# A squared-ReLU MLP by Strassen-Winograd products: two pairs interleaved in the first layer, the second layer's products taken over both token halves, sums and stores moved between queues

## The chip, the cores and the metric

The kernel runs on one core of a Trainium2 chip. The metric is the device time of one execution in microseconds (us), the median over the runs. A core has TensorE (PE, with its weight loads as PEld), VectorE (DVE), ScalarE (ACT), GpSimd (POOL) and SyncE (SP), which only issues DMAs. Each engine works through its own instructions in order; one that waits holds up all behind it. An engine that issues DMAs does so in the same order, among its other work.

## What is computed

One decoder layer over 2048 tokens of width 1024, in float32: three token mixers side by side, an output projection with residual, then an MLP, then a final norm. The change lies in the MLP and in the hand-over to it:

```python
        x = x + jnp.concatenate([ya, yb, yc], axis=-1) @ w_out[i]
        h = rmsnorm(x, norm2_g[i])
        x = x + jnp.square(jax.nn.relu(h @ w_ff1[i])) @ w_ff2[i]
    return rmsnorm(x, final_g)
```

Here `w_out` is 2048 x 1024, `w_ff1` 1024 x 4096 and `w_ff2` 4096 x 1024; `ya`, `yb` and `yc` are the mixers' results.

## The kernel before

**Products.** The tokens are worked in two halves `h` of 1024. In each layer of the MLP the product of 2x2 blocks is made with seven products `q` = 0 to 6 instead of eight, each product of operands that are blocks or sums of blocks. Every float32 operand is split into a rounded part `hi` (a cast on ACT, L902) and a rest `lo` (a subtraction on DVE, L903), and a product is three matmuls: hi*hi (L955), lo*hi (L956) and hi*lo (L957). A unit is 12 matmuls of 128x512: four steps of the inner dimension in layer 1, four row chunks in layer 2. There are 224 units in each layer and 448 x 12 = 5376 matmuls in all.

**The hand-over.** The output projection runs as four blocks (half, kb), TensorE's product tile `mmo` being added into `x` by DVE (L1026, L1036). The normed result goes to DRAM as `h2_d`. At the start of the last block `prep_x(0)` (L880) loads the sixteen blocks `xb` of half 0 (L886), makes four sums of each group of four on POOL (`t_x`, L893 to L896) and stores them to `t_d` from SP's queue (L898). `prep_x(1)` does it for half 1, one group at a time, inside layer 1.

**Layer 1.** The order is `seq1`: half, pair `j` of column blocks, product. For each pair `load_w1` (L934) loads four blocks of weights and makes four sums of them on POOL (`ws`, L939 to L942), six units ahead; `split_w1` splits them three units ahead; `load_xi` loads and splits the token operands `xr` five units ahead, those of q = 4 to 6 of half 0 at unit 2. The function `ff1` evicts a product into `p`, `u`, `v` (L1093 to L1102), makes four activations per pair (`relu2`, L1067 and L1068) and three plus one sums of these on POOL (`fs`, L1111 to L1113, L1122). The seven results of a pair go to DRAM as `f_d`, all from SP's queue (L1086).

**Layer 2.** The order is `seq2`: half, product, `k` = 0 to 15 (16 units a stage, 14 stages). `ahead2` (L1163 on) runs two units ahead and for each unit loads one block of `f_d` and makes one block of the second weights, then splits both (four engine instructions). In half 0 the weight block is loaded as it stands (q = 0, 2, 5), loaded as a sum that is already in DRAM (q = 3), or made from loaded blocks and stored to `w2t_d` (q = 1: three loads, a subtraction on POOL at L1176 and one on DVE at L1177, two stores; q = 4 at L1182 and q = 6 at L1186: two loads, one subtraction, one store). Half 1 loads everything again. At the end of a stage `evict2` takes the four banks and runs the residual, the squares and the final norm at once.

**What sets the order.** A scheduler places the instructions of each engine from the program's order, the waits of the tiles (a tile's buffers are reused in turn) and the priority that `evac` gives. So the place of a step in an engine's queue is not always its place in the text.

## Time and profile before

| what | value |
|---|---|
| median of 3 runs | 2761.77 us (2760.27 to 2762.66) |
| the profiled execution's own time | 2754.69 us |
| its span, first to last instruction | 2752.9 us |
| mean granted TensorE clock | 0.993 |
| PE busy in the span | 2665.9 us (97%) |
| DVE, ACT, POOL busy | 1720.6, 1385.0, 851.1 us (63%, 50%, 31%) |
| DMA moved | 476.22 MB, mean 173 GB/s |

The span is cut by the start times of the matmuls: the first matmul of layer 1 starts at 1441.6 us, the first of layer 2 at 2079.3 us, the last at 2742.7 us. Busy time of PE counts a matmul until its modelled end, so that a busy PE may still have gaps between starts; a stretch is best judged by how many matmuls it holds. A granted clock of 1.0 is TensorE's 2.4 GHz level, 0.5 its 1.2 GHz level; a mean between is a mixture. The profiled execution is 7.08 us below the median of the runs.

### The profile page before, as it was taken

To read this page: it belongs to the slowest core of one execution; us is meant where nothing else is said; L and a number is where in the kernel's file an instruction comes from. 1 tells how busy PE (TensorE), PEld (TensorE's weight loads), DVE (VectorE), ACT (ScalarE), POOL (GpSimd) and SP (SyncE) were. 2 spreads that over 40 slices of the span, in tenths; PEclk is the share of its full clock that TensorE was granted. 3 is DMA by queue.
4 is the path that set the end of the run, shared out by engine and by line. 5 is a ranking of instruction groups with operands and counts; after the bars stand their busy time and mean duration, and the time that the engine had idled before them with its cause. 6 is when DMAs were issued, how large, how long until landed. Compare 5 with 4: busy or idle time off the path is not lost.

```text
span 2752.9 us, 39628 instructions
## 1 busy us (share of the span) xinstructions
PE 2665.9 (97%) x14018; PEld 2218.8 (81%) x14018; DVE 1720.6 (63%) x2369; ACT 1385.0 (50%) x2565; POOL 851.1 (31%) x756
## 2 busy tenths in 40 slices
...
GB/s 118 103 129 121 147 124 99 87 127 124 123 143 107 79 159 174 204 192 245 141 137 181 201 199 176 211 168 149 160 143 257 284 279 275 301 279 207 201 213 153
DMA packets 397399, 476.22 MB, mean 173 GB/s; under 512 B 30604, under 2 KB 245360, under 8 KB 397200
## 3 DMA queue, kind: packets, MB, share of 16 engines
...
## 4 chain that ended last, share of the span: by engine, by line
PE 41%; DMA 5%; DVE 2%; POOL 2%; issue 1%; ACT 1%; SPq 1%; DVEq 0%; POOLq 0%; ACTq 0%
PE f L956 12%; PE f L957 12%; PE f L955 12%; DMA w<-in_w_ff_dram 2%; PE mmo L241 1%; PE mmo L242 1%; PE mmo L243 1%; DVE f2lo L903 1%; DMA xr<-t_d 1%; DMA w2t<-w2t_d 1%; DMA fr<-f_d 1%; POOL w2t L1176 1%; DVE xlo L903 0%; POOL w2t L1186 0%; SPq L1151 0%
## 5 line engine op out<-in xcount | busy, mean ns | idle before, releaser
L955 PE MATMUL f<-f2hi,f2hi 128*128 128x512 f32 x896 | 353.7, 395 | 20.7 <-ACT f2hi L902 15.9
L956 PE MATMUL f<-f2lo,f2hi 128*128 128x512 f32 x896 | 356.8, 398 | 10.1 <-DVE f2lo L903 10.1
L955 PE MATMUL f<-xhi,w1hi 128*128 128x512 f32 x896 | 351.9, 393 | 13.0 <-ACT xhi L902 4.4
L957 PE MATMUL f<-f2hi,f2lo 128*128 128x512 f32 x896 | 355.3, 397 | 0.0
L956 PE MATMUL f<-xlo,w1hi 128*128 128x512 f32 x896 | 351.7, 392 | 2.4 <-DVE xlo L903 2.3
L957 PE MATMUL f<-xhi,w1lo 128*128 128x512 f32 x896 | 351.0, 392 | 0.0
L528 DVE SCALAR_TENSOR_TENSOR ca<-ht,caw,ca 128x1024 f32<-128x1024 f32 x240 | 316.3, 1318 | 5.8 <-ACT ca L524 2.6
L241 PE MATMUL mmo<-whi_o,hi_y 128*128 128x256 f32 x1024 | 297.5, 291 | 13.2 <-DVE x L1026 11.4
L243 PE MATMUL mmo<-whi_o,lo_y 128*128 128x256 f32 x1024 | 290.9, 284 | 0.0
L242 PE MATMUL mmo<-wlo_o,hi_y 128*128 128x256 f32 x1024 | 290.6, 284 | 0.0
L902 ACT CAST f2hi<-fr 128x512 fp32r<-128x512 f32 x224 | 138.7, 620 | 274.5 <-PE f L956 230.0
L903 DVE TENSOR_TENSOR f2lo<-fr,f2hi 128x512 fp32r<-128x512 f32 x224 | 159.9, 714 | 185.6 <-ACT f2hi L902 185.2
L955 PEld LDWEIGHTS f<-f2hi,f2hi 128*128 128x128 f32 x896 | 170.2, 190 | 64.8 <-ACT f2hi L902 27.2
L956 PEld LDWEIGHTS f<-f2lo,f2hi 128*128 128x128 f32 x896 | 170.3, 190 | 54.6 <-DVE f2lo L903 16.5
L955 PEld LDWEIGHTS f<-xhi,w1hi 128*128 128x128 f32 x896 | 168.2, 188 | 53.8 <-ACT xhi L902 7.7
L241 PEld LDWEIGHTS mmo<-whi_o,hi_y 128*128 128x128 f32 x1024 | 195.4, 191 | 16.9 <-DVE x L1026 10.6
L956 PEld LDWEIGHTS f<-xlo,w1hi 128*128 128x128 f32 x896 | 168.2, 188 | 42.3 <-DVE xlo L903 5.2
L957 PEld LDWEIGHTS f<-f2hi,f2lo 128*128 128x128 f32 x896 | 170.6, 190 | 34.9
L957 PEld LDWEIGHTS f<-xhi,w1lo 128*128 128x128 f32 x896 | 168.2, 188 | 37.2
L242 PEld LDWEIGHTS mmo<-wlo_o,hi_y 128*128 128x128 f32 x1024 | 195.6, 191 | 1.5 <-issue 1.4
L243 PEld LDWEIGHTS mmo<-whi_o,lo_y 128*128 128x128 f32 x1024 | 195.1, 191 | 0.0
L903 DVE TENSOR_TENSOR w1lo<-ws,w1hi 128x512 fp32r<-128x512 f32 x128 | 127.0, 993 | 56.1 <-ACT w1hi L902 56.0
...
## 6 DMA issues: line engine op xcount, KB each, us to landing
w<-in_w_ff_dram SPq DMA_DIRECT2D x320, 256.0 KB, 3.6
fr<-f_d SPq DMA_DIRECT2D x224, 256.0 KB, 2.9
f_d<-fs SPq DMA_DIRECT2D x128, 256.0 KB, 2.0
w2t<-w2t_d SPq DMA_DIRECT2D x96, 256.0 KB, 3.9
...
raw_y<-y_d SPq DMA_DIRECT2D x64, 256.0 KB, 4.2
wraw_o<-in_w_out_dram SPq DMA_DIRECT2D x64, 256.0 KB, 3.6
w2t_d<-w2t SPq DMA_DIRECT2D x64, 256.0 KB, 3.1
```

The costliest lines, as they stand in the source:

```text
L241: nc.tensor.matmul(ps, lh, rh, start=(i == 0 and j == 0), stop=False)
L242: nc.tensor.matmul(ps, lh, rl, start=False, stop=False)
L243: nc.tensor.matmul(ps, ll, rh, start=False, stop=(i == n - 1 and j == len(outs) - 1))
L528: nc.vector.scalar_tensor_tensor(acc, ht[:, k:k + T], caw[:, k * 4 + t:k * 4 + t + 1], acc, op0=ALU.mult, op1=ALU.add)
L902: nc.scalar.copy(hi, raw)
L903: nc.vector.tensor_sub(lo, raw, hi.bitcast(F32))
L955: nc.tensor.matmul(ps, lh, rh, start=start and i == 0, stop=False, skip_group_check=True)
L956: nc.tensor.matmul(ps, lh, rl, start=False, stop=False, skip_group_check=True)
L957: nc.tensor.matmul(ps, ll, rh, start=False, stop=last, skip_group_check=True)
L1176: nc.gpsimd.tensor_sub(t1, b12, b11)
```

## The change

- **prep_x** loads into the four `raw` tiles of the constant pool, makes its sums in place and stores them from POOL's queue. `prep_x(0)` is spread over the first half of the last block.
- **Layer 1** takes two pairs in turn (`GRP = 2`): the order is now product by product, the two pairs in turn. The sums of the weights become `sum_w1`, five units ahead, partly in place; token operands come twelve units ahead. Of the seven stores of a pair ACT issues the three activations `f_a`, `f_b`, `f_d` and POOL the four sums.
- **Layer 2** goes product by product over both halves, so the weight block of a product is loaded and split once (`load_w2`, tile `wb`, 20 buffers) and used in both halves; all eight PSUM banks are held. Products come in the order 0, 2, 1, 3, 5, 4, 6. The sums of weights are made by `t_sums` in stages of their own (t1 in product 0's second half; t0, t2, t3 in the first halves of 2, 1 and 3), always by POOL through two `ts` tiles, and stored from POOL's queue. Residual, squares and final norm are deferred (`later`), one at every third unit. The last stage runs in two passes of two chunks.

```diff
     def prep_x(h, ks=range(4)):
 
         for k in ks:
-            b = []
-            for kk, th in ((k, 0), (k, 1), (k + 4, 0), (k + 4, 1)):
-                r = ffa.tile([P, 512], F32, tag="raw", name=f"xb_{h}_{kk}_{th}", bufs=8)
+            b11, b12, b21, b22 = b = [const.tile([P, 512], F32, tag="raw", name=f"xb_{h}_{k}_{i}", bufs=RAWB)
+                                      for i in range(4)]
+            for r, (kk, th) in zip(b, ((k, 0), (k, 1), (k + 4, 0), (k + 4, 1))):
                 nc.sync.dma_start(r, h2_d[h][kk * P:(kk + 1) * P, th * 512:th * 512 + 512])
-                b.append(r)
-            sums4(b, t_d[h], k, f"x{h}{k}", nc.gpsimd)
-
-    def sums4(b, dst, k, nm, eng):
-        b11, b12, b21, b22 = b
-        t = [ffa.tile([P, 512], F32, tag="s", name=f"t{q}_{nm}", bufs=4) for q in range(4)]
-        nc.gpsimd.tensor_sub(t[1], b12, b11)
-        eng.tensor_sub(t[0], b22, t[1])
-        nc.gpsimd.tensor_sub(t[2], b22, b12)
-        nc.gpsimd.tensor_sub(t[3], b21, t[0])
-        for q in range(4):
-            nc.sync.dma_start(dst[q, k * P:(k + 1) * P, :], t[q])
-        return t
+            nc.gpsimd.tensor_sub(b11, b12, b11)
+            nc.gpsimd.tensor_sub(b12, b22, b12)
+            nc.gpsimd.tensor_sub(b22, b22, b11)
+            nc.gpsimd.tensor_sub(b21, b21, b22)
+            for i, r in ((1, b11), (2, b12), (0, b22), (3, b21)):
+                nc.gpsimd.dma_start(t_d[h][i, k * P:(k + 1) * P, :], r)
...
-        a11, a12, a21, a22 = blk[0, 0], blk[0, 1], blk[1, 0], blk[1, 1]
-        s1, s2, s3, s4 = [ffa.tile([P, 4, P], F32, tag="s", name=f"ws{q}_{h}_{j}", bufs=4) for q in range(4)]
-        nc.gpsimd.tensor_add(s1, a21, a22)
-        nc.gpsimd.tensor_sub(s2, s1, a11)
-        nc.gpsimd.tensor_sub(s3, a11, a21)
-        nc.gpsimd.tensor_sub(s4, a12, s2)
-        WR[h, j] = [a11, s2, a12, s1, s3, s4, a22]
+        WR[h, j] = [blk[0, 0], None, blk[0, 1], None, blk[1, 0], None, blk[1, 1]]
+
+    def sum_w1(h, j, q):
+
+        w = WR[h, j]
+        a11, a12, a21, a22 = w[0], w[2], w[4], w[6]
+        if q == 1:
+            w[3], w[1] = [ffa.tile([P, 4, P], F32, tag="s", name=f"ws{i}_{h}_{j}", bufs=4) for i in range(2)]
+            nc.gpsimd.tensor_add(w[3], a21, a22)
+            nc.gpsimd.tensor_sub(w[1], w[3], a11)
+        elif q == 4:
+            nc.gpsimd.tensor_sub(a21, a11, a21)
+        elif q == 5:
+            nc.gpsimd.tensor_sub(w[1], a12, w[1])
+            w[5] = w[1]
...
-            prep_x(0)
...
+                if bi == len(blocks) - 1 and nq < 2 and c0 % 4 == 0:
+                    prep_x(0, (2 * nq + c0 // 4,))
...
-    LEADW, LEAD1, LEADX, LEAD2 = 6, 3, 5, 2
-    seq1 = [(h, j, q) for h in range(NHALF) for j in range(NPAIR) for q in range(NP)]
+    GRP = 2
+    LEADW, LEADS, LEAD1, LEADX, LEAD2, LEADB = 7, 5, 3, 12, 3, 16
+    seq1 = [(h, g * GRP + i, q) for h in range(NHALF) for g in range(NPAIR // GRP) for q in range(NP)
+            for i in range(GRP)]
...
-        for m, f in ((n + LEADW, load_w1), (n + LEAD1, split_w1)):
-            if 0 <= m < len(seq1):
-                h, j, q = seq1[m]
-                if f is split_w1:
+        for lead, f in ((LEADW, load_w1), (LEADS, sum_w1), (LEAD1, split_w1)):
+            if 0 <= n + lead < len(seq1):
+                h, j, q = seq1[n + lead]
+                if f is not load_w1:
...
-        def store(i, t):
-            nc.sync.dma_start(f_d[h][i, j * P:(j + 1) * P, :], t)
+        def store(i, t, eng):
+            eng.dma_start(f_d[h][i, j * P:(j + 1) * P, :], t)
...
+            store(0, st[j, "f11"], nc.scalar)
...
-            s1, s2, s3 = fsum(0), fsum(1), fsum(2)
+            f11, f22, f21 = st[j, "f11"], st[j, "f22"], relu2(st[j, "p1"], "c" + nm)
+            s1, s2 = fsum(0), fsum(1)
             nc.gpsimd.tensor_add(s1, f21, f22)
             nc.gpsimd.tensor_sub(s2, s1, f11)
-            nc.gpsimd.tensor_sub(s3, f11, f21)
-            store(3, s1)
-            store(1, s2)
-            store(4, s3)
-            st["s2"] = s2
+            nc.gpsimd.tensor_sub(f21, f11, f21)
+            store(3, s1, nc.gpsimd)
+            store(1, s2, nc.gpsimd)
+            store(4, f21, nc.gpsimd)
+            st[j, "s2"] = s2
         elif q == 6:
-            f12 = relu2(st["u2"], "d" + nm)
-            store(2, f12)
+            f12 = relu2(st[j, "u2"], "d" + nm)
+            store(2, f12, nc.scalar)
             s4 = fsum(3)
-            nc.gpsimd.tensor_sub(s4, f12, st["s2"])
-            store(5, s4)
+            nc.gpsimd.tensor_sub(s4, f12, st[j, "s2"])
+            store(5, s4, nc.gpsimd)
...
-        if n == 2:
+        if n == 4:
...
-        if n % NP == 3 and n // NP in (3, 5, 7, 9):
-            prep_x(1, (n // NP // 2 - 1,))
+        if n % (NP * GRP) == 6 and n // (NP * GRP) in (1, 2, 3, 4):
+            prep_x(1, (n // (NP * GRP) - 1,))
         ff1(n)
     xbs.close()
-
-
-    f2p = pool(ctx, "f2p", side="right", reuse_waits="tile")
-    seq2 = [(h, q, k) for h in range(NHALF) for q in range(NP) for k in range(NPAIR)]
-    AB = {}
+    ffst.close()
+    opst.close()
...
+    f2p = pool(ctx, "f2p", reuse_waits="tile")
+    ORDER2 = (0, 2, 1, 3, 5, 4, 6)
+    seq2 = [(q, h, k) for q in ORDER2 for h in range(NHALF) for k in range(NPAIR)]
+    LASTP = len(seq2) - NPAIR
+    FA, WB = {}, {}
...
+    def split2(r, tag, nm, bufs, n=512):
+        hi = f2p.tile([P, n], F32R, tag=tag + "hi", name=f"{tag}hi_{nm}", bufs=bufs)
+        lo = f2p.tile([P, n], F32R, tag=tag + "lo", name=f"{tag}lo_{nm}", bufs=bufs)
+        split_to(r, hi, lo)
+        return hi, lo
+
+    def load_f(u, c0=0, n=4):
+
+        q, h, k = seq2[u]
+        ra = const.tile([P, n * P], F32, tag="raw", name=f"fr_{u}_{c0}", bufs=RAWB)
+        nc.sync.dma_start(ra, f_d[h][q, k * P:(k + 1) * P, c0 * P:(c0 + n) * P])
+        FA[u, c0] = split2(ra, "fa", f"{u}_{c0}", 4, n * P)
+
+    def load_w2(u):
+        if u < len(seq2):
+            q, h, k = seq2[u]
+            if h == 0:
+                if q in (0, 2, 5):
+                    r = w2_block(*{0: (0, 0), 2: (1, 0), 5: (1, 1)}[q], k, f"{q}_{k}")
+                else:
+                    r = raw2(f"w2t_{q}_{k}", w2t_d[TI[q], k * P:(k + 1) * P, :])
+                WB[q, k] = split2(r, "wb", f"{q}_{k}", 20)
+
+    T_AT = {(0, 1): 1, (2, 0): 0, (1, 0): 2, (3, 0): 3}
+
+    def t_sums(u):
+
+        q, h, k = seq2[u]
+        i = T_AT.get((q, h))
+        if i is None:
             return
+        nm, ks = f"t{i}_{k}", slice(k * P, (k + 1) * P)
+        if i < 2:
+            x = w2_block(int(i == 0), 1, k, nm)
+            y = w2_block(0, 0, k, nm) if i else raw2(f"w2u{nm}", w2t_d[1, ks, :])
         else:
+            x = w2_block(1, int(i == 2), k, nm)
+            y = w2_block(0, 1, k, nm) if i == 2 else raw2(f"w2u{nm}", w2t_d[0, ks, :])
+        t = f2p.tile([P, 512], F32, tag="ts", name=f"ts{nm}", bufs=2)
+        nc.gpsimd.tensor_sub(t, x, y)
+        nc.gpsimd.dma_start(w2t_d[i, ks, :], t)
...
-        if q in (0, 2, 5):
-            rb = w2_block(*{0: (0, 0), 2: (1, 0), 5: (1, 1)}[q], k, nm)
-        elif h > 0 or q == 3:
-            rb = raw2(f"w2t_{nm}", w2t_d[TI[q], tsl, :])
-        elif q == 1:
-            b11, b12, b22 = w2_block(0, 0, k, nm), w2_block(0, 1, k, nm), w2_block(1, 1, k, nm)
-            t1, rb = sm(1), sm(0)
-            nc.gpsimd.tensor_sub(t1, b12, b11)
-            nc.vector.tensor_sub(rb, b22, t1)
-            nc.sync.dma_start(w2t_d[1, tsl, :], t1)
-        elif q == 4:
-            b12, b22 = w2_block(0, 1, k, nm), w2_block(1, 1, k, nm)
-            rb = sm(2)
-            nc.gpsimd.tensor_sub(rb, b22, b12)
-            b21, t2 = w2_block(1, 0, k, nm), raw2(f"w2t_{nm}", w2t_d[0, tsl, :])
-            rb = sm(3)
-            nc.gpsimd.tensor_sub(rb, b21, t2)
-        if h == 0 and q in (1, 4, 6):
-            nc.sync.dma_start(w2t_d[TI[q], tsl, :], rb)
...
+        later.append(rest)
...
+    for u in range(LASTP):
+        q, h, k = seq2[u]
+        if u + LEAD2 < LASTP:
+            load_f(u + LEAD2)
+        if u < NPAIR:
+            if u + 4 < NPAIR:
+                load_w2(u + 4)
+        else:
+            load_w2(u + LEADB)
+        t_sums(u)
+        if k % 3 == 2 and later:
+            later.pop(0)()
         if k == 0 and q in (0, 1, 4):
+            pp, tag = (ps4[0], "mm2") if h else (ps3, "mm")
+            banks[h] = [pp.tile([P, 512], F32, tag=tag, name=f"f2{q}_{h}_{c}") for c in range(4)]
+        ah, al = FA.pop((u, 0))
         for c in range(4):
             ts = slice(c * P, c * P + P)
+            mm3c(banks[h][c], [((ah[:, ts], al[:, ts]), WB[q, k])], k == 0 and q in (0, 1, 4), k == NPAIR - 1)
...
+    last = [(LASTP + k, c0) for c0 in (0, 2) for k in range(NPAIR)]
+    for u, c0 in last[:LEAD2]:
+        load_f(u, c0, 2)
+    for i, (u, c0) in enumerate(last):
+        if i + LEAD2 < len(last):
+            load_f(*last[i + LEAD2], 2)
+        if i % 3 == 2 and later:
+            later.pop(0)()
+        q, h, k = seq2[u]
+        ah, al = FA.pop((u, c0))
+        for c in range(2):
+            ts = slice(c * P, c * P + P)
+            mm3c(banks[h][c0 + c], [((ah[:, ts], al[:, ts]), WB[q, k])], False, k == NPAIR - 1)
```

Three places show what moved. In layer 1, POOL (t_x and xb are prep_x's sums, ws and w1 the weight sums of a pair, fs the sums of activations; the last digits of fs and ws name the pair). Before, around the first group of `prep_x(1)`, the sums of pairs 3 and 5:

```order
L895 TENSOR_TENSOR t2_x10_14424<-xb_1_4_1_14420,xb_1_0_1_14416 128x512
L1111 TENSOR_TENSOR fs0_0_3_14492<-f_c0_3_14488,f_b0_3_14466 128x512
L1112 TENSOR_TENSOR fs1_0_3_14493<-fs0_0_3_14492,f_a0_3_14405 128x512
L1113 TENSOR_TENSOR fs2_0_3_14494<-f_a0_3_14405,f_c0_3_14488 128x512
L896 TENSOR_TENSOR t3_x10_14425<-xb_1_4_0_14418,t0_x10_14422 128x512
L939 TENSOR_TENSOR ws0_0_5_14553<-w1_0_5_10_14549,w1_0_5_11_14551 128x512
L1122 TENSOR_TENSOR fs3_0_3_14523<-f_d0_3_14518,fs1_0_3_14493 128x512
L940 TENSOR_TENSOR ws1_0_5_14554<-ws0_0_5_14553,w1_0_5_00_14545 128x512
```

Now, behind all of the second and third group (xb_1_1, xb_1_2) and before the sums of pairs 2 and 5:

```order
L894 DMA t_d1_8402<-xb_1_2_2_14982 128x512
L889 TENSOR_TENSOR xb_1_3_0_15332<-xb_1_3_1_15333,xb_1_3_0_15332 128x512
L894 DMA t_d1_8402<-xb_1_3_0_15332 128x512
L940 TENSOR_TENSOR ws0_0_5_14448<-w1_0_5_10_14336,w1_0_5_11_14338 128x512
L941 TENSOR_TENSOR ws1_0_5_14449<-ws0_0_5_14448,w1_0_5_00_14332 128x512
L943 TENSOR_TENSOR w1_0_5_10_14336<-w1_0_5_00_14332,w1_0_5_10_14336 128x512
L890 TENSOR_TENSOR xb_1_3_1_15333<-xb_1_3_3_15335,xb_1_3_1_15333 128x512
L891 TENSOR_TENSOR xb_1_3_3_15335<-xb_1_3_3_15335,xb_1_3_0_15332 128x512
L894 DMA t_d1_8402<-xb_1_3_1_15333 128x512
L1118 TENSOR_TENSOR fs0_0_2_14407<-f_c0_2_14403,f_b0_2_14358 128x512
L892 TENSOR_TENSOR xb_1_3_2_15334<-xb_1_3_2_15334,xb_1_3_3_15335 128x512
L1119 TENSOR_TENSOR fs1_0_2_14408<-fs0_0_2_14407,f_a0_2_14244 128x512
```

The second, third and fourth group of `prep_x(1)` stand close together ahead of the sums of activations of pair 2, where before one group stood between two pairs; and POOL now issues their stores in between.

In layer 2, SP, in the stage that makes t1 (fr is the block of f_d by its unit number, w2_2 a block for the next product, w2_t1 the two operands of t1's sum). Before, in the stage of q = 1 of half 0:

```order
L1163 DMA fr_0_1_3_19999<-f_d0_8403 128x512
L1151 DMA w2_0_1_3_00_20001<-in_w_ff2_dram 128x512
L1151 DMA w2_0_1_3_01_20003<-in_w_ff2_dram 128x512
L1188 DMA w2t_d_8405<-w2t0_0_1_2_19970 128x512
L1151 DMA w2_0_1_3_11_20005<-in_w_ff2_dram 128x512
L1163 DMA fr_0_1_4_20033<-f_d0_8403 128x512
L1178 DMA w2t_d_8405<-w2t1_0_1_3_20007 128x512
```

Now:

```order
L1178 DMA fr_19_0_19809<-f_d1_8404 128x512
L1162 DMA w2_2_4_10_19943<-in_w_ff2_dram 128x512
L1162 DMA w2_t1_4_01_19949<-in_w_ff2_dram 128x512
L1162 DMA w2_t1_4_00_19951<-in_w_ff2_dram 128x512
L1178 DMA fr_20_0_19844<-f_d1_8404 128x512
```

The two stores of a unit are gone from SP's queue; three other loads stand between one f block and the next, from fr_13 on.

At the passage from layer 1 to layer 2, ACT (r and f_d are the relu and the square of the last pair, f2hi and fahi the casts of f blocks, f2hi1 and wbhi those of weight blocks). Before:

```order
L902 CAST f2hi1_0_0_1_19541<-w2_0_0_1_00_19535 128x512
L1067 ACTIVATE r_c1_15_19481<-p1_1_15_19388 128x512
L1068 ACTIVATE f_c1_15_19480<-r_c1_15_19481 128x512
L902 CAST f2hi0_0_0_2_19549<-fr_0_0_2_19545 128x512
L1067 ACTIVATE r_d1_15_19507<-u2_1_15_19407 128x512
L1068 ACTIVATE f_d1_15_19506<-r_d1_15_19507 128x512
```

Now:

```order
L1074 ACTIVATE r_d1_15_19379<-u2_1_15_19161 128x512
L1075 ACTIVATE f_d1_15_19378<-r_d1_15_19379 128x512
L1093 DMA f_d1_8404<-f_d1_15_19378 128x512
L897 CAST fahi_0_0_19396<-fr_0_0_19394 128x512
L897 CAST fahi_1_0_19402<-fr_1_0_19400 128x512
L897 CAST fahi_2_0_19408<-fr_2_0_19406 128x512
L897 CAST fahi_3_0_19439<-fr_3_0_19437 128x512
L897 CAST wbhi_0_0_19414<-w2_0_0_00_19412 128x512
```

The first weight block of layer 2 is now cast behind the last pair's activations and four casts of f blocks, where before the first units' casts stood ahead of them.

## Rows read from the trace of the kernel before

**Rows 1.** The page, costliest groups: line, engine, tiles, shapes, count | busy, mean ns | idle before.

```profile
L955 PE MATMUL f<-f2hi,f2hi 128*128 128x512 f32 x896 | 353.7, 395 | 20.7 <-ACT f2hi L902 15.9
L956 PE MATMUL f<-f2lo,f2hi 128*128 128x512 f32 x896 | 356.8, 398 | 10.1 <-DVE f2lo L903 10.1
L955 PE MATMUL f<-xhi,w1hi 128*128 128x512 f32 x896 | 351.9, 393 | 13.0 <-ACT xhi L902 4.4
```

**Rows 2.** Busy time by stretch: length, PE, PEld, DVE, ACT, POOL, PE clock, DMA share, GB/s.

```profile
1225.00:1442.00 217.00, 205.26 (x1684) 204.02 (x1683) 100.99 (x176) 72.47 (x178) 44.95 (x41) 0.98 0.55 179
1442.00:1495.00 53.00, 47.24 (x201) 36.18 (x201) 31.82 (x47) 31.41 (x58) 22.14 (x17) 1.00 0.62 199
1495.00:1715.00 220.00, 220.00 (x960) 179.88 (x959) 118.60 (x137) 110.15 (x181) 155.30 (x108) 1.00 0.58 191
1715.00:1815.00 100.00, 90.42 (x388) 71.77 (x387) 71.49 (x83) 60.34 (x104) 55.09 (x38) 1.00 0.61 202
2079.00:2480.00 401.00, 370.15 (x1543) 293.85 (x1542) 229.28 (x330) 165.83 (x303) 87.41 (x68) 0.97 0.83 283
2126.00:2196.00 70.00, 54.14 (x194) 38.49 (x193) 27.53 (x43) 17.35 (x31) 15.43 (x12) 0.93 0.83 283
2334.00:2356.00 22.00, 22.00 (x98) 18.06 (x97) 16.06 (x25) 14.42 (x29) 0.00 (x0) 1.00 1.05 384
2480.00:2743.00 263.00, 263.00 (x1150) 215.56 (x1148) 145.77 (x227) 113.31 (x211) 5.35 (x9) 1.00 0.61 193
```

**Rows 3.** Timeline of the end: start, us, engine.

```profile
2742.72 0.40 PE L957 MATMUL f<-f2hi,f2lo 128*128 128x512 f32 x1
...
2749.78 0.33 SPq L1230 DMA_DIRECT2D out_dram<-v  x1
```

**Rows 4.** Waits, output projection 1225 to 1442: total us, times, longest.

```profile
POOL t_x L893 <- DMA xb<-h_d: 27.9, 3, 10.9
...
DVE w1lo L903 <- ACT w1hi L902: 16.8, 2, 8.4
ACT w1hi L902 <- POOL ws L940: 10.2, 1, 10.2
PE mmo L241 <- DVE x L1026: 9.9, 4, 3.6
```

**Rows 5.** Waits of SP's queue, 1225 to 2079 (layer 1 and before).

```profile
SPq L1086 <- POOL fs L1111: 117.9, 30, 6.1
```

**Rows 6.** Groups of instructions of POOL, whole span: an issue of a DMA.

```profile
L736 POOL DMA_DIRECT2D zs_d<-zt x32 | 18.3, 572 | 85.7 <-ACT zt L734 84.0 <-DVE ca L528 1.6
```

**Rows 7.** Groups of instructions in layer 1, 1495 to 1715, POOL.

```profile
L942 POOL TENSOR_TENSOR ws<-w,ws 128x512 f32<-128x512 f32 x12 | 20.9, 1744 | 0.0
...
L1111 POOL TENSOR_TENSOR fs<-f_c,f_b 128x512 f32<-128x512 f32 x11 | 16.9, 1538 | 0.0
...
L893 POOL TENSOR_TENSOR t_x<-xb,xb 128x512 f32<-128x512 f32 x4 | 5.2, 1293 | 7.2 <-DVE w1lo L903 3.5 <-issue 2.7 <-POOL ws L942 1.0
```

**Rows 8.** DMA issues, 2126 to 2196: count, KB each, median us to landing.

```profile
w2t_d<-w2t SPq DMA_DIRECT2D x25, 256.0 KB, 3.4
fr<-f_d SPq DMA_DIRECT2D x15, 256.0 KB, 4.2
```

**Rows 9.** Groups of instructions in layer 2, 2079 to 2480.

```profile
L903 DVE TENSOR_TENSOR f2lo<-fr,f2hi 128x512 fp32r<-128x512 f32 x131 | 95.7, 731 | 79.0 <-ACT f2hi L902 78.6
L902 ACT CAST f2hi<-fr 128x512 fp32r<-128x512 f32 x131 | 81.1, 619 | 134.8 <-PE f L956 92.3 <-DMA fr<-f_d 37.0 <-issue 3.3
...
L1186 POOL TENSOR_TENSOR w2t<-w,w2t 128x512 f32<-128x512 f32 x16 | 27.8, 1742 | 60.8 <-DMA w2t<-w2t_d 52.6 <-issue 5.9 <-DVE f2lo L903 2.3
...
L1177 DVE TENSOR_TENSOR w2t<-w,w2t 128x512 f32<-128x512 f32 x16 | 11.1, 693 | 43.7 <-POOL w2t L1176 32.9 <-DMA w<-in_w_ff_dram 10.8
```

**Rows 10.** Waits of SP's queue, 2079 to 2480 (layer 2).

```profile
SPq L1178 <- POOL w2t L1176: 44.8, 16, 3.8
SPq L1188 <- POOL w2t L1186: 33.1, 15, 4.4
```

132 lines of the change are left out of this document (58 added, 74 removed).

## The prediction

> **What bounds the kernel now.** I read the page's costliest groups first: nearly all of the MLP's time is TensorE's, and what TensorE waits for there is an operand's cast or its remainder, in layer 2 more than in layer 1 [rows 1]. Then the busy time by stretch, for where these waits lie [rows 2]. A stretch without a gap sets the floor: 960 matmuls in 220.00 us, that is 2.75 us a unit of twelve and 44.0 us for sixteen units; 1150 matmuls in 263.00 us say the same. Against it, in us lost:
>
> - output projection, 1225 to 1442: 217.00 - 205.26 = 11.7 idle, and the clock of 0.98 is another 4.3: 16.
> - start of layer 1, 1442 to 1495: 53.0 - 44.0 = 9.
> - from half 0 to half 1 of layer 1, 1715 to 1815: 100.0 - 88.0 = 12.
> - first eight stages of layer 2, 2079 to 2480: 401 - 352 = 49, of which 26 in the stage that makes two sums per unit (2126 to 2196, 70 for 44).
> - the rest of the MLP: nothing; the end after the last matmul: 2742.7 to about 2753, 10 [rows 3].
>
> So 96 us can be had at most. The profiled execution (2754.69 us; its span leaves 1.8 us around it) lies 7.1 us under the median; the sum is made against it and 7.1 added.
>
> **Output projection.** The waits there [rows 4]: TensorE waits 9.9 us for DVE's `x`, and not because DVE is busy: DVE waits twice 8.4 us for a cast of layer 1's weights, one of which waits 10.2 us for POOL's weight sums, and POOL stands 27.9 us at `prep_x`'s loads, ahead of these sums. The scheduler had put `prep_x(0)` early. The new one takes the constant pool's tiles, which it gets only when the last block's operands have left them, and POOL has the weight sums of the first pairs ahead of it. The cause goes; layer 1's first casts remain in DVE's queue among the evictions, so I keep 3 of the 16 (bounds 0 and, if both 8.4 us waits stay but the third is gone, 11). Gain 13.
>
> **Start of layer 1 and its half change.** Operands of the next product were loaded five units ahead, and those of q = 4 to 6 at unit 2, when their loads queue up; now twelve units (33 us) ahead, four of them even at the start, where interleaving gives each product two units. DVE is busy 71.49 of 100 us in the half change [rows 2], so the work fits if it is spread. From 9 to 1 and from 12 to 2: gain 8 and 10; bounds no gain in either and 9 and 12.
>
> **Stores on the producers' queues.** SP waited 117.9 us in layer 1 for the first sum alone [rows 5], with weight loads behind it, yet TensorE ran without a gap there: gain nothing. POOL pays: 4 issues a pair at 0.572 us [rows 6] are 2.3 us in 19.3 (seven units). On ACT, whose issue of such a store no row shows, I take SP's 0.33 [rows 3], at most POOL's: 1.0 to 1.7 us a pair; ACT was busy 110.15 of 220 [rows 2], which covers it.
>
> **prep_x(1) in layer 1.** POOL was busy 155.30 of 220 us [rows 2]. The scheduler now puts the second to fourth group close together, ahead of the weight sums of pair 5 and the activation sums of pair 2. Through four raw tiles a group needs four subtractions at 1.29 [rows 7], four issues at 0.572 and then, before the next can begin, a store's landing and a reload. Landings are 3.4 and 4.2 [rows 8], partly beside the other subtractions: about 10 to 12 us a group. From the first sum of pair 1's last product at unit 13 (+41 us of layer 1) on, adding these rounds and the sums between, POOL finishes `fs1` of pair 2 at +89.5 with no other hold-up, +95 if each reload also waits in SP's order. ACT's square of the next pair needs that tile, and the eviction behind it on ACT is due at unit 32, +88.8. I take a new stall of 6, between 0 (the sums turn out ahead) and 25 (each of three groups holds 8 more).
>
> **Passage to layer 2.** The first weight cast of layer 2 now stands behind the last pair's activations. From the last matmul of layer 1: its end 0.4, eviction 0.7, two activations, a store's issue, four f casts, the weight cast and its remainder: 7 of ACT's at 0.619, 0.33, 0.731 [rows 3, 9] = 6.5 us. What was lost there before is part of the 49. Bounds 4 (the casts slip in ahead) and 8.2, with the clock's half level for 3.4 us after.
>
> **Layer 2's traffic.** Before, half 0 lost its time at SP, which waited 44.8 and 33.1 us for POOL's and DVE's sums before it could issue their stores [rows 10], with the f loads behind. Those stores leave SP. Each weight block is loaded once instead of twice; of the transfers (256 KB each) 224 + 288 + 64 stores become 224 + 112 + 128 + 64, 48 fewer, but crowded: per unit, in this order of stages, 2, 5, 2+2 and so on: (first product, half 0) f and w, 2; (half 1) f, w, two for t1 and its store, 5; (second product, half 0) f, two, a store, 4; (half 1) 2; then 4, 2, 4, 2. From f_13 on SP's queue has the extra loads; that block can be issued at unit 5, eight ahead (four raw, four split). Up to f_47 that is 35 units, 96 us, with 35 f + 32 + 16 loads and 16 stores for the second stage, and 32 + 16 for the third: 147 transfers, 38.5 MB. At the 330 GB/s that I put between 283 (the starved stage) and 384 (a stretch of loads, DMA share 1.05) [rows 2], because here one in five is a store, it takes 117 us: 21 too long, of which the stock of f blocks covers 12 (eight units, 22 us, less a landing of 4.2 [rows 8], a split of 1.35 [rows 9] and a unit or two for their place in SP's order). Left 9; with the stages behind it 12. At 384: 100 us, 4 too long, covered: 0. At 283: 136 us, 40 - 12 = 28, and up to 43 over all stages.
>
> The Trainium skill ("DMA: Bandwidth & Descriptors", section Specifications) gives 358 GB/s as the limit of a core's memory; by that figure the same sum is 108 us and nothing is left over, 12 us less than forecast. The 384 of our trace already lies above it, so the measured ends are kept.
>
> So layer 2: from 49 to 6.5 + 12, gain 30.5. From unit 128 on, two transfers a unit at most, as in the 263 us without a gap: nothing. ACT and DVE split fewer weights: they were not the limit.
>
> **The end.** Two chunks instead of four follow the last matmul: from 10 to 7.5, gain 2.5.
>
> **Sum.** 13 + 8 + 10 - 6 + 30.5 + 2.5 = 58: 2754.7 - 58 = 2696.7, plus 7.1: **2704 us**.
>
> **Rivals.**
>
> 1. *The transfers decide.* They go at 283 GB/s whenever loads and stores mix, as in the stage of 2126 to 2196: layer 2 loses 30 us more than forecast, 2734. For it: a DMA share of 0.83 is all that this stretch reached [rows 2]. Against: SP was held there by POOL's sums, so it was not a test of the rate. The Trainium skill ("DMA: Bandwidth & Descriptors", section Issuing engines are not separate DMA queues) says that issuing on more engines saves only the issue time, as all share the same 16 DMA engines; no run here shows that side, while the trace shows the 44.8 us of waiting in SP's order that the move does away with.
> 2. *POOL's backlog in layer 1 is large*: 25 instead of 6: 2723.
> 3. *Nothing is lost anew*: transfers at 384, no backlog, passage 4, and all of 16, 9 and 12 back: 2704 - 12 - 6 - 2.5 - 6 = 2678.
> 4. *POOL's sums become layer 2's limit, and it is slower.* One of q = 1's sums ran on DVE at 0.693; now all are POOL's at up to 1.742 [rows 9]. Through two `ts` tiles, two sums cost one subtraction, one issue and one landing in sequence: (1.742 + 0.572 + 3.4)/2 = 2.86 us a unit against 2.75, which the stock covers. A longer landing holds POOL, hence the `wr` tiles, hence SP and the f blocks. All else as forecast (38 - 12 = 26 us lost) leaves 96 - 26 = 70 us to lose before it is slower: with 12 of stock, over four stages of 16 units, 1.28 us a unit, so it decides from a landing of 5.7 us. At 7 us: 1.91 x 64 - 12 - 70 = 40 beyond: 2802. Against: the longest median here is 4.2 [rows 8]. The Trainium skill ("GPSIMD Engine Reference", section 4.1 Engine selection) advises against POOL for such sums, about twice slower than DVE; the rows have 2.5 times.
> 5. *It does little*: the first rival's worst (43) with the second: 2754; within 0.2% only by chance.
>
> **How the numbers follow.** 0.2% (5.5 us) is about what a measurement of this kernel can tell from no change. Forecast (2690 to 2718) 0.43; first rival 0.20; second 0.13; third 0.11; fourth 0.08; fifth 0.05. The range drops the fourth, half of the fifth and the end of the third: 2682 to 2748. Faster 0.88, same 0.04, slower 0.08.
>
> **What would show it.** Right: no wait of `mmo` for DVE's `x` in the output projection; the start of layer 1 near 44 us for sixteen units; a gap of TensorE some 85 to 100 us into layer 1, behind ACT waiting for POOL's `fs` or `ws`; 6 to 7 us between the last matmul of layer 1 and the second of layer 2; gaps from the second half of product 0 on, with the DMA share over 0.9 and f casts waiting for f loads, and none from the fifth product on. Wrong: SP's queue waiting mostly for POOL's `ts` (fourth rival); layer 1 with gaps beyond its first 120 us; a DMA share under 0.85 while f loads are late.

## The result and the profile after

The changed kernel takes 2778.92 us, the median of 4 runs (2773.74 to 2785.19), against 2761.02 us (2756.38 to 2762.66, 4 runs) for the kernel before on the same chip. The ratio is 1.0069, with a 95% interval of 1.0044 to 1.0093: **it is slower by 0.7%**, where 2704 us was forecast. The profiled execution after takes 2773.74 us (span 2772.0) and the one before 2754.69 us (span 2752.9), 19 us apart, so it is these two that are compared below.

All 5376 matmuls of the MLP are in both traces, so the loss of every unit can be taken from their start times. Units are numbered 0 to 223 in layer 1 and 224 to 447 in layer 2, and a unit without a gap takes 2.7475 us (the gap-free units of both kernels). "Loss" below is the length of some units less 2.7475 us each. The sum of the differences is the whole 19 us:

| stretch | before | forecast | after |
|---|---|---|---|
| start of layer 1 (its first matmul) | 1441.6 | 1428.6 | 1445.2 |
| loss of units 0 to 15, start of layer 1 | 9.1 | 1 | 1.0 |
| units 16 to 31, `prep_x(1)` | 0.1 | 6 | 18.8 |
| units 96 to 127, half change | 11.8 | 2 | 14.4 |
| units 208 to 239, passage to layer 2 | 3.3 | 6.5 | 12.2 |
| units 240 to 351, the stages with sums | 45.2 | 12 | 40.3 |
| units 352 to 447 | -0.1 | 0 | -2.6 |
| from the last matmul to the end of the span | 10.2 | 7.5 | 10.8 |

Seen from TensorE's groups on the page of the changed kernel (columns as in [rows 1]; `wb` and `fa` are the new names of layer 2's weights and activations), the idle time ahead of layer 2's first product of each three has grown (from 20.7 us in [rows 1]), and it is mostly ACT's cast that ends it:

```profile
L958 PE MATMUL f<-wbhi,fahi 128*128 128x512 f32 x896 | 354.1, 395 | 34.3 <-ACT fahi L897 29.1
```

The busy time by stretch of the changed kernel (columns as in [rows 2]), cut where its own stages lie:

```profile
1225.00:1445.00 220.00, 205.24 (x1685) 204.22 (x1685) 94.55 (x176) 71.73 (x178) 53.95 (x59) 0.96 0.55 175
1445.00:1489.00 44.00, 44.00 (x199) 36.14 (x198) 27.47 (x42) 25.83 (x50) 15.99 (x14) 1.00 0.69 215
1489.00:1552.00 63.00, 51.73 (x199) 38.76 (x197) 31.69 (x27) 22.06 (x38) 50.95 (x50) 0.92 0.57 188
1715.00:1819.00 104.00, 94.63 (x393) 75.72 (x392) 81.28 (x86) 57.94 (x102) 62.50 (x53) 0.95 0.59 194
...
2158.00:2208.00 50.00, 45.65 (x192) 35.23 (x191) 18.05 (x26) 16.73 (x30) 21.72 (x22) 1.00 0.88 297
2208.00:2337.00 129.00, 114.67 (x481) 91.58 (x479) 46.35 (x62) 36.73 (x70) 53.80 (x58) 0.95 0.89 300
...
2479.00:2743.00 264.00, 264.00 (x1166) 218.61 (x1165) 127.60 (x202) 94.44 (x188) 18.14 (x28) 1.00 0.50 153
```

The start of layer 1 is as forecast: 44 us without a gap. The output projection has 14.8 us idle instead of 11.7. Right behind the start comes a new hole of 11.3 us of idle, in which POOL is busy for 51 of 63 us; the granted clock of 0.92 there adds to it. The stretch from 2208 to 2337 (most of the stage that makes t0, the one behind it and the first half of the t2 stage) has 14.3 us idle at a DMA share of 0.89. From 2479 on nothing is lost.

**Output projection.** The waits from 1225 to 1445 after the change (total us, times, longest; answers [rows 4]), of PE, DVE, ACT and of SP's queue:

```profile
PE mmo L243 <- DVE x L1041: 13.2, 4, 8.0
...
DVE wlo_o L233 <- ACT whi_o L232: 27.3, 9, 9.4
ACT whi_o L232 <- DMA wraw_o<-in_w_out_dram: 22.1, 6, 9.6
...
SPq L888 <- DMA t_d<-xb: 27.0, 12, 5.3
```

Read it from the bottom. SP stands at the loads of the next `xb` group (L888), because the four raw tiles are still being stored to `t_d`. Behind it in SP's queue are the weight blocks `wraw_o` of the output projection. Their cast on ACT waits 9.6 us, the remainder on DVE waits 9.4 us for the cast, DVE's evictions into `x` stand behind that, and TensorE waits 8.0 us for a bank (at 1360; a second stop of 4.7 us, start to start, is at 1395). Before, POOL and layer 1's weights stood at the head of this chain; now it is SP and the projection's own weights.

**Units 16 to 31.** POOL's timeline (start, us, engine, line; in brackets the idle time before and what ended it) and the waits from 1489 to 1556:

```profile
1527.09 1.26 POOL L889 TENSOR_TENSOR xb<-xb,xb 128x512 f32<-128x512 f32 x1 [4.87 <-DMA xb<-h_d]
...
1533.95 1.09 POOL L894 DMA_DIRECT2D t_d<-xb  x2
1539.81 1.28 POOL L889 TENSOR_TENSOR xb<-xb,xb 128x512 f32<-128x512 f32 x1 [4.76 <-DMA xb<-h_d]
...
1542.13 1.25 POOL L940 TENSOR_TENSOR ws<-w,w 128x512 f32<-128x512 f32 x1 [0.19 <-DMA w<-in_w_ff_dram]
```

```profile
ACT w1hi L897 <- POOL ws L941: 17.6, 3, 6.4
...
PE f L958 <- ACT w1hi L897: 7.8, 3, 3.6
```

One group of `prep_x(1)` follows the other at 12.7 us (1527.09 to 1539.81). The last stores of a group are issued at 1535.0 and the next sum starts at 1539.8: store landed, tile free, reload, first sum. POOL only waits in that time, and `ws` of the next pair stands behind.

ACT is held a second way, by its own stores. The square `f_b` is done at 1520.1 us, but its store is issued only at 1528.45, right after an `xb` load of SP's queue has landed; in the trace the store waits for the landing semaphore that it shares with that load. The weight cast behind it reads no `xb` and is late with it:

```profile
1528.45 0.33 ACTq L1093 DMA_DIRECT2D f_d<-f_b  x1
1528.82 0.62 ACT L897 CAST w1hi<-w 128x512 fp32r<-128x512 f32 x1 [8.67 <-DMA xb<-h_d]
```

Three stores wait so in units 16 to 31, for 5.9, 8.3 and 4.7 us, and TensorE's longest gap there, 3.8 us at unit 28, ends with this cast.

**Half change.** SP's timeline from 1690 on, and waits of ACT and TensorE from 1715 to 1832:

```profile
1691.53 57.85 SPq L929 DMA_DIRECT2D w<-in_w_ff_dram  x11
1749.47 1.88 SPq L916 DMA_DIRECT2D xr<-t_d  x4
```
```profile
ACT xhi L897 <- DMA xr<-t_d: 10.3, 3, 9.1
...
PE f L960 <- DVE w1lo L898: 5.3, 2, 4.1
```

For 58 us SP issues eleven weight loads of layer 1, each when a tile comes free, and only then the first sums of half 1. ACT reaches their cast early and holds the weight casts behind it for 9.1 us. TensorE has gaps of 4.2 us at units 104 and 116. The first ends with the cast of such a load. The second ends with DVE's remainder `w1lo`, which stands behind four remainders of `xr` at 1.67 us each while POOL makes sums:

```profile
1789.20 6.68 DVE L898 TENSOR_TENSOR xlo<-xr,xhi 128x512 fp32r<-128x512 f32 x4
```

**Passage.** ACT and DVE behind the last evictions of layer 1:

```profile
2098.66 0.33 ACTq L1093 DMA_DIRECT2D f_d<-f_d  x1
2099.02 2.18 ACT L897 CAST fahi<-fr 128x512 fp32r<-128x512 f32 x4 [0.40 <-ACT f_d L1075]
2101.11 2.69 ACT L897 CAST wbhi<-w 128x512 fp32r<-128x512 f32 x5
```
```profile
2099.68 6.57 DVE L898 TENSOR_TENSOR falo<-fr,fahi 128x512 fp32r<-128x512 f32 x4 [2.42 <-ACT fahi L897]
2106.17 3.09 DVE L898 TENSOR_TENSOR wblo<-w,wbhi 128x512 fp32r<-128x512 f32 x5
```

The casts come in the order that the prediction read. But the first remainder of a weight block stands behind four remainders of `f` blocks on DVE, at 1.64 us each where [rows 9] had 0.731. TensorE stands for 5.4 us ahead of the first matmul of layer 2 and for 4.9 us behind it.

**Layer 2.** The chain of work that ended last, from 2204 on, in order of time (start, us, what; `tst` are the `ts` tiles); from 2204.88 to 2250 the same four steps repeat:

```profile
2204.88 5.96 DMA w2t_d<-tst
2210.84 0.08 issue
2210.92 1.29 POOL tst L1207
2212.21 0.29 issue
2212.49 4.58 DMA w2t_d<-tst
```

Waits of POOL and of SP's queue from 2107 to 2479, and the median landing of the store there (64 of them, from POOL's queue, 256 KB):

```profile
POOL tst L1207 <- DMA w2t_d<-tst: 42.5, 37, 3.3
...
SPq L1162 <- POOL tst L1207: 112.6, 60, 4.0
```

```profile
w2t_d<-tst POOLq DMA_DIRECT2D x64, 256.0 KB, 4.8
```

With two `ts` tiles every second sum waits until the store of the sum before last has landed. That is two sums in 1.28 + 0.3 + 4.8 = 6.4 us, 3.2 us a unit where TensorE needs 2.75: 7 us in a stage of 16 units, 28 in the four that make sums, of the 41.7 that these lose. SP then waits 112.6 us for POOL to free the `wr` tiles of the operands, with the f loads behind. SP waited for POOL before, too ([rows 10], 44.8 + 33.1 us); the wait has changed its place, not gone.

### The profile page after: what moved, and what is told of

Its sections match the earlier page's. It is cut to its first block, busy times and chain, and to the rows that moved or that the text cites. A ratio compares the mean times of both kernels' runs of the same rounds, so it can differ in the third digit from the quotient of the medians.

```text
span 2772.0 us, 39031 instructions
## 1 busy us (share of the span) xinstructions
PE 2666.1 (96%) x14018; PEld 2225.3 (80%) x14018; DVE 1679.5 (61%) x2257; ACT 1321.5 (48%) x2469; POOL 985.4 (36%) x996
## 5 line engine op out<-in xcount | busy, mean ns | idle before, releaser
L958 PE MATMUL f<-wbhi,fahi 128*128 128x512 f32 x896 | 354.1, 395 | 34.3 <-ACT fahi L897 29.1
L959 PE MATMUL f<-wblo,fahi 128*128 128x512 f32 x896 | 352.8, 394 | 4.3 <-DVE wblo L898 4.3
L960 PE MATMUL f<-wbhi,falo 128*128 128x512 f32 x896 | 353.3, 394 | 1.0 <-DVE falo L898 0.7
L898 DVE TENSOR_TENSOR falo<-fr,fahi 128x512 fp32r<-128x512 f32 (+1 forms) x240 | 168.1, 705 | 279.2 <-ACT fahi L897 262.9
L897 ACT CAST fahi<-fr 128x512 fp32r<-128x512 f32 (+1 forms) x240 | 140.9, 591 | 345.1 <-PE f L959 277.5
L958 PEld LDWEIGHTS f<-wbhi,fahi 128*128 128x128 f32 x896 | 170.8, 191 | 73.9 <-ACT fahi L897 33.5
L958 PEld LDWEIGHTS f<-xhi,w1hi 128*128 128x128 f32 x896 | 170.1, 190 | 55.8 <-ACT w1hi L897 10.9
L960 PEld LDWEIGHTS f<-wbhi,falo 128*128 128x128 f32 x896 | 170.4, 190 | 40.9 <-DVE falo L898 5.8
L959 PEld LDWEIGHTS f<-wblo,fahi 128*128 128x128 f32 x896 | 170.6, 190 | 40.5 <-DVE wblo L898 4.8
L898 DVE TENSOR_TENSOR w1lo<-w,w1hi 128x512 fp32r<-128x512 f32 x128 | 142.9, 1122 | 70.4 <-ACT w1hi L897 70.4
```

The lines of the kernel that those rows point to most:

```text
L897: nc.scalar.copy(hi, raw)
L898: nc.vector.tensor_sub(lo, raw, hi.bitcast(F32))
L958: nc.tensor.matmul(ps, lh, rh, start=start and i == 0, stop=False, skip_group_check=True)
L959: nc.tensor.matmul(ps, lh, rl, start=False, stop=False, skip_group_check=True)
L960: nc.tensor.matmul(ps, ll, rh, start=False, stop=last, skip_group_check=True)
```

## The experiments

Fourteen kernels ran. Single runs stand to the changed kernel's own 2773.74 to 2785.19 us, so for them the loss by units says more than the total. Letters are those of the expectations, which were written before each run.

**More `ts` tiles.** Two tiles become six.

```diff
-        t = f2p.tile([P, 512], F32, tag="ts", name=f"ts{nm}", bufs=2)
+        t = f2p.tile([P, 512], F32, tag="ts", name=f"ts{nm}", bufs=6)
```

> The changed kernel with six tiles ts instead of two. Theory A (the chain subtraction, issue, landing through two tiles limits POOL): before this edit two sums take 6.35 us, 3.17 a unit against 2.75; with six tiles POOL takes a subtraction and an issue, about 1.9 us a unit, so that the 41.7 us lost in the four stages that make sums (5.8, 18.8, 8.1, 9.0) fall to 15 or less, and the time to about 2750. Theory B (the transfers are the limit, 3 to 5 of 256 KB a unit): the same bytes in the same units, so the loss stays within 8 us of 41.7 and the time at 2770 to 2780.

2755.91 us. The four stages that lost (units 240 to 271, 288 to 303 and 320 to 335) went from 41.7 to 21.6 us, and POOL's waits for its own stores are gone. What is left is in SP's queue, from 2107 to 2479:

```profile
SPq L1162 <- POOL tst L1207: 86.9, 58, 3.5
```

Theory A has the cause and not the size: its 15 us or less were not reached. The `ts` ring is half of the loss; the six `wr` tiles of the operands are next, since a tile is held from its load to POOL's sum.

**The sums on DVE.** Same tiles, `nc.gpsimd.tensor_sub(t, x, y)` becomes `nc.vector.tensor_sub(t, x, y)`; the stores stay with POOL.

> The changed kernel with the weight sums of layer 2 subtracted by DVE instead of POOL; stores still from POOL's queue, still two tiles. Theory A (the chain through two tiles): only the subtraction shortens, 1.28 to 0.69, so a unit takes (0.69 + 0.3 + 4.8) / 2 = 2.9 instead of 3.17; the 41.7 us lost in the four stages fall by some 10 to 17, not to nothing. Theory C (POOL's slow arithmetic is the limit): 3.17 falls under 2.75 and the stages lose under 10. Theory B (transfers): no change beyond 5 us.

2762.03 us; the four stages lose 30.3 us. A sum takes 0.69 instead of 1.3 us, and the loss falls by 11.4, about half of what six tiles gave. DVE now waits 43.7 us for the stores to land. That is in theory A's range, and far from theory C's. So the sum's duration is one part of the round trip and the landing the larger one.

**Wider rings in both places.** `ts` from 2 to 4 and `wr` from 6 to 8, which costs fewer tiles than six and six.

> The changed kernel with four tiles ts and eight wr instead of two and six, so the same total as six and six. Theory A (two rings in turn: behind the tiles ts stands the ring of wr tiles, through which SP waits 46.8 us for POOL's sums between 2140 and 2260): the four stages that make sums lose less than the 21.6 us of six and six, 14 or less, most of it in the t0 stage. Rival B (past the ts ring the transfers are the limit, 358 GB/s at a share of 1.00 in 2200 to 2250): 19 to 25 us as with six and six.

2737.83 us; the four stages lose 9.7 us of the 41.7, as theory A has it (though not most of it in the t0 stage, 4.3 us). SP's wait and the busy time of the t1 stage:

```profile
SPq L1162 <- POOL tst L1207: 37.9, 32, 2.8
```
```profile
2158.00:2208.00 50.00, 50.00 (x223) 41.39 (x222) 22.23 (x28) 17.73 (x31) 30.43 (x32) 1.00 1.02 378
```

Where the changed kernel had 297 GB/s and gaps (row of 2158 above), the same loads and stores now go at 378 GB/s without a gap. The transfers had not been the limit; the rings had.

**t1 one stage earlier**, on top of that: `T_AT = {(0, 0): 1, ...}` in place of `(0, 1)`.

> Four ts and eight wr tiles, and t1 made in product 0's first half, so that no two stages with sums follow each other (5, 2, 4, 2, 4, 2, 4, 2 transfers a unit instead of 2, 5, 4, 2, 4, 2, 4, 2). Rival B (transfers): the 147 transfers in 35 units are spread over two more stages, so the sum of all losses in the first eight stages of layer 2 falls by 8 us or more against the run with four and eight. Theory A (rings alone): within 4 us of it, the loss only moves to the first stage.

2735.55 us; the first eight stages lose 11.3 instead of 14.9 us, within theory A's 4 us.

**`xb` loads of `prep_x(0)` from POOL's queue**, so that SP's weight loads don't stand behind them.

```diff
-                nc.sync.dma_start(r, h2_d[h][...])
+                (nc.gpsimd if h == 0 else nc.sync).dma_start(r, h2_d[h][...])
```

> The changed kernel with the sixteen loads xb of prep_x(0) issued from POOL's queue instead of SP's. Theory D (SP waits for the landing of a store to t_d before the next xb load, and the weight loads of the output projection stand behind it): the gaps of 8.3 and 4.7 us in the output projection go, with the 10 and 7 us at half clock behind them, and layer 1 starts near 1430 instead of 1445. Rival E (DVE's queue holds the first casts of layer 1 ahead of the evictions, whatever SP does): layer 1 still starts within 4 us of 1445.

2781.75 us. Layer 1 starts at 1448.7, which is within the 4 us of rival E, but not for its reason, and theory D falls. The stall has moved and become one: TensorE stands for 17.6 us at 1385.8. Waits from 1380 to 1406 and SP's longest:

```profile
PE mmo L243 <- DVE x L1042: 17.3, 1, 17.3
...
ACT whi_o L232 <- DMA wraw_o<-in_w_out_dram: 10.4, 1, 10.4
ACT hs L849 <- DMA h_d<-hs: 8.2, 1, 8.2
...
SPq L917 <- DMA t_d<-xb: 28.3, 4, 24.2
```

POOL stands at its own loads, its stores of `h_d` wait behind them and ACT waits for these; on SP the `xr` loads now wait 24.2 us for the raw tiles, with the last weights behind. With the four raw tiles going round through DRAM, a queue stood in both arrangements.

**`prep_x(1)` in other tiles.** Its blocks go into the six `fs` tiles instead of the raw tiles of the constant pool.

```diff
-            b11, ... = b = [const.tile([P, 512], F32, tag="raw", ..., bufs=RAWB)
+            b11, ... = b = [const.tile([P, 512], F32, tag="raw", ..., bufs=RAWB) if h == 0 else
+                            fwp[0].tile([P, 512], F32, tag="fs", ..., bufs=6)
```

> The changed kernel with the blocks xb of prep_x(1) in the tiles of the activation sums instead of the constant raw tiles. These come free in the program's order, so the four groups stand one to every two pairs in POOL's queue instead of three close together. Theory F (three rounds through four tiles in a row hold POOL): the loss of 18.8 us in units 16 to 31 of layer 1 falls under 4 and does not come back later. Rival G (POOL has more to do than time, the stores issued from its queue included): the loss spreads over the next groups, 12 us or more in units 16 to 96 in all.

2761.78 us. Units 16 to 31 lose 0.0 instead of 18.8 us and the rest of layer 1 is unchanged (23.5 in all). Theory F holds, and this settles that stall. ACT's waits at its stores are gone with it. Two things changed at once, six tiles for four and the sums of activations taking turns in them; which of them does it was not tried apart.

**Half 0's blocks in tiles of their own as well** (those of `p1`, `u2` and `v`, free in the output projection), on top of the last.

> As the run with xb of half 1 in the activation sums' tiles, and xb of half 0 in the six tiles of layer 1's accumulators, which lie idle until layer 1. Loads again from SP. Theory D' (what holds the output projection is the ring of four raw tiles that xb shares with the operands: SP waits at a load until a store to t_d has landed or an operand is split, with the projection's weight loads behind it): the gaps of 7.3 and 4.4 us of that run go, and layer 1 starts at 1436 or before instead of 1447.7. Rival E' (the scheduler now places prep_x(0) early as in the kernel before, ahead of layer 1's weight sums on POOL, and DVE waits at the first casts): layer 1 starts near the 1441.6 of the kernel before, with gaps around 1270 to 1305.

2759.4 us; layer 1 starts at 1444.2. SP waits 10.9 us for the stores of `xb` instead of 27.0, yet TensorE has gaps of 7.1 us at 1267 and 3.8 us at 1281. The wait that the trace of the changed kernel names is shorter, and the gain of 13 us is still not there. Rival E' is borne out: before both gaps DVE waits for casts of layer 1's weights (24.8 us in three waits, the longest 11.2), with the evictions into `x` behind, as in the kernel before.

**All wider rings together**: `ts` 4, `wr` 8, t1 early, `prep_x(1)` in the `fs` tiles.

> Four ts and eight wr tiles, t1 in product 0's first half, and xb of half 1 in the activation sums' tiles; xb of half 0 as in the changed kernel. If the stalls are separate (theories A and F together): the time of the run with t1 early, 2735.6, less the 18 us of units 16 to 31, so 2717, 1.6% below the kernel before. If they share a cause or one uncovers the next: 2725 or more.

2717.03 us (2716.55 to 2721.04, 4 runs), 0.9847 times the kernel before (0.9831 to 0.9864). The two repairs add up, as expected: the stalls in layer 1 and layer 2 are separate.

**And half 0's blocks in the eight weight tiles of layer 1**, as in the kernel before.

```diff
-   const.tile([P, 512], F32, tag="raw", name=f"xb_{h}_{k}_{i}", bufs=RAWB) if h == 0 else
+   ffa.tile([P, 512], F32, tag="raw", name=f"xb_{h}_{k}_{i}", bufs=8) if h == 0 else
```

> The same, with xb of half 0 in the eight raw tiles of layer 1's weights, from which the first weights must then wait. Theory D' (the shared ring of four tiles holds SP, and DVE waits for casts that were placed too early): POOL has all of prep_x(0) ahead of the weight sums and SP no load behind a store, so layer 1 starts at 1436 or before and the time is 2709 or less. Rival E' (as in the kernel before, where the same tiles were used: weight casts wait for POOL and hold DVE): layer 1 starts at 1440 to 1446, and the time is within 5 us of the run with three rings.

**2713.98 us** (2712.79 to 2715.34, 4 runs), ratio 0.9837 (0.9822 to 0.9852): 1.6% faster than the kernel before, and the lowest median here; the run above and the two four-run kernels below lie within noise of it or little above. Layer 1 starts at 1440.6, about as before the change, which is in the range of rival E' and not of theory D'. The waits from 1225 to 1445:

```profile
ACT whi_o L232 <- DMA wraw_o<-in_w_out_dram: 19.2, 3, 14.5
DVE wlo_o L233 <- ACT whi_o L232: 18.3, 6, 12.4
...
PE mmo L243 <- DVE x L1032: 10.4, 3, 8.8
...
SPq L889 <- DMA h_d<-hs: 11.8, 1, 11.8
```

The projection's own weights arrive late again, now for another reason. With tiles to spare the `xb` loads stand so early in SP's queue that one waits 11.8 us for a block of the normed result that is still on its way to DRAM. Three arrangements gave starts of 1440.6 to 1448.7; none gave the 1428 of the forecast. What the projection could gain, and how, stays open.

**Half change: `xr` of half 1 from ACT's queue** (`(nc.scalar if h else nc.sync).dma_start(raw, src)` in `load_xi`).

> The changed kernel with the token operands xr of half 1 loaded from ACT's queue instead of SP's. Theory H (in the half change these loads stand behind weight loads on SP, which wait up to 24 us for tiles; ACT waits 9.1 us for one of them with a weight cast behind): the 14.4 us of units 96 to 127 fall to 7 or less. Rival I (the ring of four raw tiles and the order of casts on ACT set the pace, whoever issues): 11 to 17 us remain.

2795.98 us. The gap at unit 104 is gone, but units 111 to 115 have gaps of up to 6.5 us, units 96 to 127 lose 20.1 and units 16 to 47 lose 34.4 us. Theory H falls in this form. For units 16 to 47 the trace shows why: the first of these loads already stand in ACT's queue at 1546, and ACT waits 11.9 us there, for a sum of POOL that frees a raw tile, with a weight cast behind; TensorE stands for 9.0 us. That the same holds the half change is likely, but was not shown apart.

**A shorter lead for `xr`**: `LEADX` 12 becomes 8.

> The changed kernel with the token operands loaded 8 units ahead instead of 12. Theory K (at 12 units the casts of half 1's operands stand on ACT ahead of the weight casts of pairs 14 and 15, and wait there for loads that come one ring of four tiles at a time; TensorE stops at units 104 and 116): with 8 the stop at 104 goes and the 14.4 us of units 96 to 127 fall to 9 or less. Rival I (the ring of four raw tiles sets the pace from unit 99, when the first old operand comes free): the stops move behind unit 112 and 12 us or more remain. The start of layer 1, where 12 units were the gain, may lose up to 8 again.

2780.2 us; the half change loses 16.3 us, with the gap at unit 104 still 4.4 us. Theory K falls; the size is rival I's. The start of layer 1 still loses only 1.0 us, so its gain does not hang on the long lead. A shorter lead in the program does not repair the half change.

**First weight block first.** Layer 2's first weight block goes into a raw tile of the constant pool and is loaded and cast ahead of the f blocks.

```diff
+                if u == 0:
+                    r = const.tile([P, 512], F32, tag="raw", name="w2_0_0", bufs=RAWB)
+                    nc.sync.dma_start(r, wff2[0:P, 0:512])
...
     for u in range(LEAD2):
+        if u < 1:
+            load_w2(u)
         load_f(u)
```

> The changed kernel with layer 2's first weight block loaded into a constant raw tile, so that its cast stands ahead of the f casts instead of behind four of them. Theory J (before the first unit's third product ACT makes five casts and DVE five remainders, four of these at 1.64 us instead of 0.73 as POOL sums at the same time): the gap of 4.9 us after layer 2's first matmul falls to 2 or less and the 12.2 us of units 208 to 239 to 9 or less. Rival L (what counts is the chain from the last product over eviction, relu, square, store): the loss stays within 2 us of 12.2.

2767.79 us. The gap of 4.9 us behind the first matmul of layer 2 is gone, 1.5 us stand behind the second, and units 208 to 239 lose 8.2 instead of 12.2, as theory J has it. DVE's timeline shows the exchange:

```profile
2100.99 1.07 DVE L898 TENSOR_TENSOR wblo<-w,wbhi 128x512 fp32r<-128x512 f32 x1 [2.42 <-ACT wbhi L897]
2101.99 5.62 DVE L898 TENSOR_TENSOR falo<-fr,fahi 128x512 fp32r<-128x512 f32 x3
```

**The same on top of the best kernel.**

> The kernel of three wider rings and prep_x(0) in the weight tiles (2713.98 us), with the first weight block of layer 2 loaded into the constant pool and cast ahead of the f casts. Theory J (the passage's gap is the place of that cast in ACT's order, and adds to the other repairs): the gap behind the first matmul of layer 2 falls from about 5 to 1.5 us and the 32 units around the passage lose about 8 instead of 12; the time is 4 us less, 2710 us. Rival: what stands behind (the f splits of units 1 to 3) is late next, because all of them come out of the same queue of DVE; then the passage moves and the time stays within 1.5 us of 2714.

2715.72 us (2714.39 to 2718.16), ratio 0.9828: the same as without it. The gap behind the first matmuls falls from 6.5 to 1.5 us as theory J has it, but units 208 to 239 lose 11.5 instead of 13.1, not 8, and units 224 to 255 lose 11.9 us, where the best kernel lost 8.4: a new gap of 2.7 us at unit 242. (The two profiled executions lie 5.4 us apart, the medians 1.7, so a part of this is the choice of execution.) What stands there is not what either theory named. Busy time and a wait of this kernel:

```profile
2090.00:2140.00 50.00, 48.92 (x202) 36.42 (x200) 17.34 (x26) 17.67 (x30) 29.06 (x32) 1.00 1.05 402
```
```profile
ACT fahi L898 <- DMA fr<-f_d: 27.0, 12, 6.0
```

With the rings wide enough the t1 stage runs at 402 GB/s for 50 us, and f casts wait for f loads. Five transfers of 262 KB a unit, 1.31 MB, take 3.26 us at that rate. **Here the transfers bind** by their rate, at a DMA share of 1.05, and what is won ahead of this stage is lost in it; no run took transfers out of this stage alone to prove it.

**Half 1's first weight loads from POOL's queue**, on top of that.

```diff
-                nc.sync.dma_start(r, wff1[...])
+                (nc.gpsimd if h and j < GRP else nc.sync).dma_start(r, wff1[...])
```

> As the run before it, with the loads of layer 1's weights for the first two pairs of half 1 issued from POOL's queue instead of SP's. What is open is what holds the half change, 14 us in all kernels with the change. Theory M: SP's weight loads, which wait for tiles (24 us in one stretch), stand ahead of the xr loads of half 1; without them xr arrives in time and units 96 to 127 lose 9 us or less; 2705 us. Rival N: the raw tiles of xr come free only as ACT casts, so the loads stay late, and POOL now waits for weight tiles ahead of its own sums: units 96 to 127 lose 12 or more, and ACT waits for POOL's fs or ws tiles; 2710 us or more.

2717.66 us (2714.09 to 2718.59), ratio 0.9834, no change; units 96 to 127 lose 13.8 us. SP's timeline and wait (1690 to 1790):

```profile
1718.51 7.87 SPq L917 DMA_DIRECT2D xr<-t_d  x4
```
```profile
SPq L917 <- DVE xlo L899: 42.4, 20, 18.7
```

The loads of half 1 start at 1718.5, 31 us earlier than in the changed kernel; ACT's longest wait for them is 2.9 us and the gap at unit 104 is gone. So theory M named what held the loads, but its 9 us did not come: the loss is now spread over units 107 to 116, and SP waits for the raw tiles that DVE's remainders free. Rival N's size came true; its late loads and its waits of ACT for POOL did not show. What the trace shows in their place is DVE: from 1730 to 1780 it is busy for 44.0 of 50 us, its remainders of `xr` take 1.10 us each where 0.69 is the time without POOL's sums, and TensorE's longest wait for an operand is for `w1lo` (4.3 us in two waits). No run made DVE faster there, so the 14 us of the half change stay without a repair.

## Why the prediction was wrong, point by point

The forecast was a gain of 58 us; the trace shows a loss of 19. By the prediction's own steps (gains in us):

| step | forecast | measured |
|---|---|---|
| output projection | 13 | -3.7 |
| start of layer 1 | 8 | 8.1 |
| half change | 10 | -2.6 |
| `prep_x(1)` in layer 1 | -6 | -18.7 |
| passage and layer 2 | 30.5 | -1.5 |
| the end | 2.5 | -0.6 |

- **"Layer 2's traffic"** is the step that failed most: with the passage it is 32 us of the 77 by which the sum is off (units 240 to 351 were to lose 12 and lost 40.3). It took the f loads' lateness as a matter of GB/s, 330 between 283 and 384, and let SP's waits go because the stores leave SP (it named POOL's and DVE's sums there; both [rows 10] name POOL's). The wait is the ring's and went along to POOL: two `ts` tiles, a landing, and the six `wr` tiles behind them. That is the **fourth rival**, which had 0.08. Its formula gives the pace: with the measured 1.28, 0.3 and 4.8 us, 3.2 us a unit, where the prediction had 2.86 and let the stock cover it. The landing of 3.4 us was taken from SP's stores in a starved stage [rows 8]; in the stages that it is about, POOL's took 4.8. It does not give all of the size: 28 us of the 41.7, less still with the stock of 12; what the formula lacks is the second ring behind it (six `ts` tiles alone left 21.6 us). The kernel is slower though the landing stayed below the rival's threshold of 5.7, because the other gains that it allowed for were not there either. The sign that the prediction gave for it came (SP's queue waited 112.6 us for POOL's `ts`), the one of a DMA share under 0.85 did not (0.89 from 2208 to 2337). The pair of wider rings (41.7 to 9.7 us) shows it, and the 378 GB/s beside it refute the first rival.
- **The passage** was right in its order of casts on ACT and wrong on DVE: it counted one remainder of 0.73 us, but four of `f` blocks at 1.64 us each stand ahead of the weight block's. The loss grew by 8.9 us. Forecast were 6.5, bounded by 4 and 8.2 with the half clock; measured were 12.2. Casting the weight block first took 4 of them.
- **`prep_x(1)`**: the rounds of subtractions, stores, landing and reload and the engine (POOL, with `ws` and `fs` behind) were right; a group was put at 10 to 12 us and took 12.7. The stall was mis-sized, 6 for 18.8, within its bound of 25. The sum had POOL finish `fs1` of pair 2 at +89.5 to +95 us of layer 1; it finished at +108.5. And it went by one path, `fs` and ACT's square, for which ACT waited only 3.2 us: TensorE was stopped by weight casts, late for `ws` (17.6 us of waits) and behind ACT's own stores, with gaps from 71 to 106 us into layer 1 where the text expected one at 85 to 100.
- **Output projection**: "the cause goes" was read from POOL's wait alone. POOL's wait for the `xb` blocks was one way to hold a cast back; with four raw tiles the same loads hold SP's queue, and the projection's own weights are in it. The bound (0 to 11 us left of 16) had no room for a larger loss than before. Three rearrangements left layer 1's start between 1440.6 and 1448.7 us.
- **Half change**: "the work fits if it is spread" counted DVE's busy time. Loads came late, held in SP's queue by weight loads that wait for tiles; a lead of twelve units did not bring them forward. But with these loads 31 us earlier (last run) the loss was still 13.8 us, and DVE, slowed beside POOL's sums, ended TensorE's longest waits for operands, as it ended the gap at unit 116 in the changed kernel. So the loads are the first cause and not the only one; what would give the 10 us back stays open.
- **The start of layer 1** was right to 0.1 us, its reason only in part: with a lead of 8 units the loss is 1.0 us too, so the twelve that the prediction counted on were not needed. What the interleaving does for it was not tried apart.
- **The end**: the last store is issued 5.1 us after the last matmul starts, against 7.1 before [rows 3], so 2 of the 2.5 us came. But the span ends 5.7 us after that issue, where it was 3.1 before. No view used here says why, and it was not tried.
- **Stores on the producers' queues** were put at nothing. The issue itself takes ACT 0.33 us, as put; the term left out is the wait before it, 18.9 us of ACT in three stores of units 16 to 31. It hangs on the `xb` loads: with `prep_x(1)` in other tiles the three waits are gone, so it is a part of that stall and not a second one.
